# Encoder layer with a routed mixture of experts: combine weights applied per slot, residual built by accumulating DMAs, two experts combined by one-hot matmuls

## The chip, the cores and the metric

The kernel runs on one core of a Trainium2 chip. The metric is the device time of one execution in microseconds (us), the median of several runs; lower is better.

## The reference, cut to what matters

512 tokens of width 1024 pass through a gated attention and gating stage, a cross-attention over 256 memory rows, a mixture of 16 experts and a last normalization. The change touches the mixture and what follows it. Each token picks one group of four experts and two experts in it; an expert is a SwiGLU block of inner width 512, and its output is scaled by a combine weight of the token:

```python
ew = jax.nn.softmax(evals, axis=-1) * gval
expert_id = gidx * EXPERTS_PER_GROUP + eidx
combine = jnp.sum(jax.nn.one_hot(expert_id, N_EXPERTS) * ew[..., None], axis=1)
for e in range(N_EXPERTS):
    he = jax.nn.silu(t @ w_gate[e]) * (t @ w_up[e])
    y = y + combine[:, e:e + 1] * (he @ w_down[e])
...
return rms_norm(x, g_final)
```

## The kernel before, in words

All engines follow an order written out by hand (a manual schedule): each engine runs its instructions in the order in which the program records them, and a wait holds back all that stands behind it on that engine.

**One expert.** Up to 128 rows of an expert's tokens are gathered from `h3d` in HBM. Precision comes from splitting each fp32 operand into a high part (`h`, made by ScalarE, L128) and a low part (`l`, the difference, made by VectorE or, for one of twelve pieces of an expert, by GpSimd, L129) and running three matmuls (L237 to L239). An expert has six weight chunks of 1 MB (gate 0 and 1, up 2 and 3, down 4 and 5), each in two halves; each half feeds six matmuls of 128x512. `W.pump` converts the next half whenever a half has been used, six slots ahead; `W.issue` loads chunks into raw slots as these come free.

**A period.** `expert_period(e)` records the gate and up matmuls of expert e (`gate_up`, eight halves; hooks (j, i) run small work after chunk j, half i), then the transposes of the next expert's rows (`xtr`: eight transposes `pt_xt` in two banks, copied to `xh` and `xl`), then the down matmuls of expert e-1 (`down_scatter`: four halves into `y`, which is scattered to `ybuf` in HBM by an indirect DMA of GpSimd, L1205). Hook (0, 1) transposes the SwiGLU result of expert e-1 (`h_e`: `pt_h`, `hh`, `hl`). For the row numbers of an expert, VectorE builds a one-hot matrix (`oh_e`, L1171), four small matmuls contract it with `vals` (`ids_e`, L1178), and VectorE writes `ixall` (L1179), whose columns are the row in `h3d` and the row in `ybuf`. Row numbers are made four experts ahead and gathers three ahead. All transposes and the `ids` results use the two PSUM banks of tag T in turn: a new one waits until the one two before it has been read.

**The end.** A token's two outputs lie in a low and a high row of `ybuf`, unscaled. After the scatter of expert 14, four loads of 1 MB bring `ybuf` back (`yt`, L1385); ScalarE, GpSimd and VectorE scale and add the low half into the residual `xr`; for the high half eight groups of matmuls add `yt` (through an fp32 identity, L1435) and expert 15's output (through its transposed one-hot `ohT`, L1439, L1440), and VectorE scales by `whi` and adds (L1444). Sums of squares, a reciprocal root by small VectorE steps (L253 to L282, in two chains), products by GpSimd (L1453) and the stores follow. `combine_weights` (14 small VectorE operations) stands in expert 5's period.

Of the kernel before, what the change touches and what calls it, by code (L numbers as in the profile page):

```python
# [12 lines left out]
I32 = mybir.dt.int32  # L13
# [20 lines left out]
AHEAD = 4  # L34
# [8 lines left out]
def encoder(ctx, tc, x, mem, wf, we, wr, br, gv, gcol, gqk, rope, lngb, wsT, bs, out):  # L43
# [1172 lines left out]
    def ids_e(e):  # L1216
        ixs[e] = ids(f"e{e}", ohs[e], lambda t: vals[:, t, e, :], ixall[:, e])
# [3 lines left out]
    W.limit = len(W.order) - 1  # L1221
# [5 lines left out]
    ids_e(1)  # L1227
# [7 lines left out]
    wlo = rt_([P, NT], "wlo")  # L1235
    whi = rt_([P, NT], "whi")
# [7 lines left out]
    def combine_weights():  # L1244
# [43 lines left out]
    def down(e, evac, pumps=(1, 1, 1, 1)):  # L1288
        for n in range(2):
            c = cid[e, 4 + n]  # L1290
            ps = bank("F", f"y{n}_e{e}")
# [9 lines left out]
    def down_scatter(e, pumps=(1, 1, 1, 1)):  # L1301
        if e == 4:
            yt = W.take("y12", [P, 2, D])
            ys.extend(yt[:, i] for i in range(2))
        y = ys[e % len(ys)]
        down(e, lambda n, ps: A.activation(y[:, n * 512:(n + 1) * 512], ps, AF.Copy), pumps)  # L1306
        s_ = scatter(f"e{e}", y, ixs[e])
# [9 lines left out]
    def expert_period(e):  # L1317
        gu_banks(e)
        if e == 5:
# [5 lines left out]
        def oh_ids(n, a, b):  # L1325
            hooks[a].append(lambda: oh_e(n))
            hooks[b].append(lambda: ids_e(n))

        if e == 0:
            def second():  # L1330
                ids_e(2)
                gather(ixs[2], xes[0])

            hooks[0, 0] = [lambda: oh_e(2)]
            hooks[2, 0] += [counts]
            hooks[2, 1] = [second, lambda: oh_e(3)]
# [16 lines left out]
        if e + 3 < NE:  # L1353
# [329 lines left out]
```

## Time and profile before

| what | value |
|---|---|
| median of 3 runs | 792.25 us (792.01 to 792.33) |
| profiled execution, its own time | 791.65 us |
| span of its trace | 789.9 us |
| PE (TensorE matmul) busy | 738.5 us, 93% |
| PEld (weight load) busy | 615.0 us, 78% |
| DVE (VectorE) busy | 610.6 us, 77% |
| ACT (ScalarE) busy | 462.9 us, 59% |
| POOL (GpSimd) busy | 183.7 us, 23% |
| moved by DMA | 163.72 MB, 207 GB/s |

The span is divided into what happens up to 457 us (all before the experts), the expert periods from 457 to 752.8 us, and the end from there to 789.9 us. The share of busy time is a mean over all of it; what an edit is worth has to be read from the stage in which it stands. An engine's idle time is named with the event that ended it.

### The profile page before, as it was taken

Reading aid. Unit: us, or ns where it says so; the run is one execution under the profiler, and the core shown is the slowest. Engines: PE = TensorE matmul, PEld = TensorE weight load, DVE = VectorE, ACT = ScalarE, POOL = GpSimd, SP = SyncE. Lnnn points to the kernel's source line nnn. Section 1 sums busy time; section 2 is a strip of 40 time slices with the busy share of each in tenths; the row PEclk is TensorE's granted clock in tenths of the full one; section 3 lists DMA queues with packets and bytes.
Section 4 is the critical chain, followed back from the end, with each engine's and each line's share of the span. In section 5 each row is a group of like instructions: output and inputs, shape, how many; then the busy total and the mean of one; then the engine's idle time right before and its main releaser. Section 6 shows DMA issues by size and latency. Waiting matters only on the chain.

```text
span 789.9 us, 10636 instructions
## 1 busy us (share of the span) xinstructions
PE 738.5 (93%) x3895; PEld 615.0 (78%) x3896; DVE 610.6 (77%) x1030; ACT 462.9 (59%) x703; POOL 183.7 (23%) x133
## 2 busy tenths in 40 slices
PE   4987999999999999999999989999999999999990
PEld 3775899778888888889988867888788878888760
DVE  5869899989563424658776878899999999999765
ACT  4544767665422323235555446888788888888732
POOL 4425322222000010102222120333333333322131
PEclk9989999999999999999999999999999999999996
DMA  7303221111133326436634369999899999993352
GB/s 285 134 1 126 88 107 54 55 54 54 54 106 107 107 102 244 138 115 254 245 107 187 134 246 420 420 419 396 326 398 370 372 365 373 380 379 133 108 216 110
DMA packets 28813, 163.72 MB, mean 207 GB/s; under 512 B 5077, under 2 KB 5109, under 8 KB 12496
## 3 DMA queue, kind: packets, MB, share of 16 engines
q1 hardware_dynamic: 20384, 140.52, 46.3%
q0 software_dynamic: 7360, 19.29, 6.7%
q10 hardware_dynamic: 1008, 3.15, 1.0%
q8 instruction: 33, 0.54, 0.3%
q14 instruction: 28, 0.23, 0.1%
HBM read 154.63 MB, written 16.25 MB: 216 GB/s over the span
## 4 chain that ended last, share of the span: by engine, by line
PE 71%; DVE 17%; ACT 6%; issue 3%; DMA 2%; SPq 0%; DVEq 0%; ACTq 0%
PE u_e L237 4%; PE y_e L237 3%; PE y_e L239 3%; PE y_e L238 3%; PE u_e L238 3%; PE u_e L239 3%; PE g_e L238 3%; PE g_e L237 3%; PE g_e L239 3%; PE g L238 3%; PE g L239 3%; PE g L237 3%; DVE l_e L129 2%; PE y L238 2%; PE y L239 2%
## 5 line engine op out<-in xcount | busy, mean ns | idle before, releaser
L129 DVE TENSOR_TENSOR l_e<-r_e,h_e 128x1024 fp32r<-128x1024 f32 x174 | 222.0, 1320 | 26.4 <-ACT h_e L128 26.3
L128 ACT ACTIVATE h_e<-r_e 128x1024 fp32r<-128x1024 f32 x188 | 191.9, 1055 | 24.5 <-PE u_e L239 12.5
L1183 POOL DMA_INDIRECT xe<-h3d,ixall x15 | 23.0, 1535 | 139.7 <-PE pt_xt_e L296 90.6
L237 PE MATMUL g_e<-h_e,xh_e 128*128 128x512 f32 x124 | 50.9, 411 | 0.0
L237 PE MATMUL u_e<-h_e,xh_e 128*128 128x512 f32 x124 | 50.7, 409 | 0.0
L238 PE MATMUL g_e<-l_e,xh_e 128*128 128x512 f32 x124 | 49.5, 400 | 0.8 <-DVE l_e L129 0.8
L238 PE MATMUL u_e<-l_e,xh_e 128*128 128x512 f32 x124 | 49.5, 399 | 0.0
L239 PE MATMUL u_e<-h_e,xl_e 128*128 128x512 f32 x124 | 49.5, 399 | 0.0
L239 PE MATMUL g_e<-h_e,xl_e 128*128 128x512 f32 x124 | 49.4, 399 | 0.0
L237 PE MATMUL y_e<-h_e,hh_e 128*128 128x512 f32 x120 | 48.7, 406 | 0.7 <-ACT hh_e L231 0.7
L239 PE MATMUL y_e<-h_e,hl_e 128*128 128x512 f32 x120 | 47.5, 396 | 0.0
L238 PE MATMUL y_e<-l_e,hh_e 128*128 128x512 f32 x120 | 47.4, 395 | 0.0
L580 ACT ACTIVATE p<-s,nm,qsc 128x512 f32<-128x512 f32 x32 | 25.1, 784 | 35.5 <-DVE nm L577 20.4
L129 POOL TENSOR_TENSOR l_e<-r_e,h_e 128x1024 fp32r<-128x1024 f32 x14 | 33.5, 2396 | 51.2 <-ACT h_e L128 51.2
L1306 ACT ACTIVATE y<-y_e 128x512 f32<-128x512 f32 x30 | 18.0, 600 | 22.6 <-PE y_e L239 22.6
L1205 POOL DMA_INDIRECT ybuf<-y,ixall x15 | 25.5, 1697 | 24.2 <-ACT y L1306 22.1
L238 PEld LDWEIGHTS g_e<-l_e,xh_e 128*128 128x128 f32 x124 | 23.6, 191 | 6.1 <-DVE l_e L129 1.2
L239 PEld LDWEIGHTS g_e<-h_e,xl_e 128*128 128x128 f32 x124 | 23.6, 190 | 6.1 <-DVE xl_e L232 0.4
L239 PEld LDWEIGHTS u_e<-h_e,xl_e 128*128 128x128 f32 x124 | 23.6, 190 | 5.7
L238 PEld LDWEIGHTS u_e<-l_e,xh_e 128*128 128x128 f32 x124 | 23.6, 190 | 5.0
L237 PEld LDWEIGHTS g_e<-h_e,xh_e 128*128 128x128 f32 x124 | 23.7, 191 | 5.0
L237 PEld LDWEIGHTS u_e<-h_e,xh_e 128*128 128x128 f32 x124 | 23.6, 190 | 5.0
(451 smaller groups left out, 2159.9 us busy)
## 6 DMA issues: line engine op xcount, KB each, us to landing
r_e<-in_we_dram SPq DMA_DIRECT2D x95, 1024.0 KB, 9.1
r_a<-in_wf_dram SPq DMA_DIRECT2D x4, 1024.0 KB, 5.0
r_b<-in_wf_dram SPq DMA_DIRECT2D x4, 1024.0 KB, 4.7
r_y<-in_wf_dram SPq DMA_DIRECT2D x4, 1024.0 KB, 4.8
r_wo<-in_wf_dram SPq DMA_DIRECT2D x4, 1024.0 KB, 4.8
ybuf<-zt POOLq DMA_DIRECT2D x2, 2048.0 KB, 12.8
yt<-ybuf SPq DMA_DIRECT2D x4, 1024.0 KB, 10.9
xt<-in_x_dram SPq DMA_DIRECT2D x4, 512.0 KB, 7.5
```

Source lines behind the costliest of these rows:

```text
L128: A.activation(h, rr, AF.Copy)
L129: lo = lambda X=G if onpool >> i & 1 else V, l=l, rr=rr, h=h: X.tensor_tensor(l, rr, h, op=ALU.subtract)
L237: T.matmul(ps, ah, bh, start=first and i == 0, stop=False)
L238: T.matmul(ps, ah, bl, start=False, stop=False)
L239: T.matmul(ps, al, bh, start=False, stop=last and i == n - 1)
L580: A.activation(pr, ps, AF.Exp, bias=nm, scale=qsc[t][:, h:h + 1], accum_out=sx)
L1183: G.indirect_dma_start(out=xe, out_offset=None, in_=h3d, in_offset=bass.IndirectOffsetOnAxis(ap=ix[:, 0:1], axis=0), bounds_check=S - 1, o ...
L1205: return G.indirect_dma_start(out=ybuf, out_offset=bass.IndirectOffsetOnAxis(ap=ix[:, 1:2], axis=0), in_=y, in_offset=None, bounds_check=2 ...
L1306: down(e, lambda n, ps: A.activation(y[:, n * 512:(n + 1) * 512], ps, AF.Copy), pumps)
```

## The change

- The combine weight is applied per slot of an expert (`wsl`, one column per expert) when `y` leaves PSUM, by the scale operand of that copy. The weights travel through the `ids` matmuls: `vals` gets three more fp16 columns (a weight in three pieces), and `slot_weights` adds the pieces by four small VectorE operations.
- `combine_weights` (now 6 operations) and `weight_tables` (17 small GpSimd operations) stand in expert 1's period. Experts 0 to 3 (`NLATE`) have had their row numbers before that: their `y` stays in one of three buffers, and two periods later `late` builds the one-hot again, contracts it (`weight_of`), scales `y` on ScalarE and scatters it.
- Row numbers are made and rows gathered two experts ahead, both at hook (2, 1) of a period.
- After expert 13's scatter eight DMAs of 512 KB on GpSimd's queue add `ybuf` into `xr` (`accum_op`), first the low rows and then the high ones. The loads `yt`, the scatter of expert 14, the identity matmuls and the scaled adds are gone.
- Experts 14 and 15 are both combined by one-hot matmuls. Expert 14's part for the columns 0 to 511 is put ahead of and between the transposes of expert 15's SwiGLU result. One chain of reciprocal-root steps serves all four row tiles; the products that GpSimd made are made by VectorE.

```diff
-    def ids(name, oh, val_t, ix):
+    def slot_weights(name, pi, e):
+        sw = sm.tile([P, 3], F32, tag="sw", bufs=2, name=f"sw_{name}")
+        V.tensor_copy(sw, pi[:, 2:5])
+        for i in (1, 0):
+            V.scalar_tensor_tensor(sw[:, i:i + 1], sw[:, i + 1:i + 2], 1.0 / WK, sw[:, i:i + 1], op0=ALU.mult, op1=ALU.add)
+        V.tensor_scalar(wsl[:, e:e + 1], sw[:, 0:1], 1.0 / WS, None, op0=ALU.mult)
+
+    def ids(name, oh, e, ix, n=2):
         pi = bank("T", f"ids_{name}")
         for t in range(NT):
-            T.matmul(pi[:, :2], oh[:, t], val_t(t), start=t == 0, stop=t == NT - 1)
+            T.matmul(pi[:, :n], oh[:, t], vals[:, t, e, 0:n], start=t == 0, stop=t == NT - 1)
         V.tensor_scalar(ix, pi[:, 0:2], BIGI, None, op0=ALU.add)
+        if n > 2:
+            slot_weights(name, pi, e)
...
+    def weight_of(e):
+        pi = bank("T", f"wt_e{e}")
+        for t in range(NT):
+            T.matmul(pi[:, 2:5], ohs[e][:, t], vals[:, t, e, 2:5], start=t == 0, stop=t == NT - 1)
+        slot_weights(f"e{e}", pi, e)
...
+    def late(e):
+        weight_of(e)
+        A.activation(ye[e], ye[e], AF.Copy, scale=wsl[:, e:e + 1])
+        y_scatter(e)
...
+        def ids_g(n, k=5):
+            ids_e(n, k)
+            gather(ixs[n], xes[n % 2])
         if e == 0:
...
-            hooks[2, 1] = [second, lambda: oh_e(3)]
-            hooks[3, 0] = [lambda: ids_e(3), lambda: xT.update({1: xtr("e1", xes[1], xslot)}), lambda: oh_e(0)]
-        elif e + AHEAD < NE:
...
-        if e == 5:
-            hooks[3, 1] = [combine_weights]
+            hooks[2, 1] = [lambda: ids_g(2, 2), lambda: oh_e(3)]
+            hooks[3, 0] = [lambda: xT.update({1: xtr("e1", xes[1], xslot)})]
+            hooks[3, 1] = [lambda: oh_e(0)]
+        elif e == 1:
+            hooks[0, 0] += [lambda: ids_g(3, 2)]
+            hooks[1, 0] += [lambda: ids_e(0, 2)]
+            hooks[1, 1] += [combine_weights, weight_tables]
+        elif e + 2 < NE:
+            hooks[0, 1].append(lambda: oh_e(e + 2))
+            hooks[2, 1].append(lambda: ids_g(e + 2))
+        if 2 <= e < 2 + NLATE:
+            hooks[1, 0].append(lambda: oh_e(e - 2))
+            hooks[3, 0].append(lambda: late(e - 2))
         if e == NE - 2:
             W.climit = 2 * cid[e, 4] + 3
+            hooks[1, 1].append(lambda: oh_tr(0))
...
+    for i in range(2):
         for t in range(NT):
+            G.dma_start(xr[:, t, :], ybv[t][:, i], accum_op=ALU.add)
     h_e(E - 1)
...
-    down_scatter(E - 1, (1, 1, 0, 0))
+    down(E - 1, evac(0), (1, 1, 0, 0))
...
-        nc.sync.dma_start(yt, ybv[t])
...
+    def comb(t, n, i):
+        cs = slice(n * 512, (n + 1) * 512)
+        for j in range(2):
+            T.matmul(yc[t, n], ohT["t"][:, i, t], yhl[i][:, j, cs], start=i == 0 and j == 0, stop=i == 1 and j == 1)
...
     for i in range(2):
+        comb(2 * i, 0, 0)
+        comb(2 * i + 1, 0, 0)
...
-        V.scalar_tensor_tensor(xr[:, t, cs], yc[n, t], whi[:, t:t + 1], xr[:, t, cs], op0=ALU.mult, op1=ALU.add)
+        V.tensor_tensor(xr[:, t, cs], yc[t, n], xr[:, t, cs], op=ALU.add)
+        A.activation(sqj[:, cs], xr[:, t, cs], AF.Square, accum_out=ssf[:, n, t:t + 1])
...
+    V.tensor_tensor(yos[3], xr[:, 3, :], gfin, op=ALU.mult)
+    V.tensor_tensor(ssf[:, 0], ssf[:, 0], ssf[:, 1], op=ALU.add)
+    rs = rsqrt(ssf[:, 0], 1.0 / D, EPS, NT, "fin")
+    store(3, rs[:, 3:4], True, q=A)
+    store(0, rs[:, 0:1])
+    store(1, rs[:, 1:2])
+    store(2, rs[:, 2:3], n=2)
```

What this moves stands below at three places. First VectorE at the end of expert 0's period, where expert 1's rows are transposed (`ixall` is the reading of a row-number bank, `xl` that of a transpose bank). Before:

```order
L1179 TENSOR_SCALAR ixall<-ids_e_4718 128x2
L1171 TENSOR_TENSOR oh_e_4727<-io_3529,posm 128x512
L129 TENSOR_TENSOR l_e_1_4736<-r_e_1_4221,h_e_1_4735 128x1024
L1179 TENSOR_SCALAR ixall<-ids_e_4741 128x2
L232 TENSOR_TENSOR xl_e_4748<-pt_xt_e_4749,xh_e_4747 128x512
```

Now:

```order
L1190 TENSOR_SCALAR ixall<-ids_e_4717 128x2
L1171 TENSOR_TENSOR oh_e_4726<-io_3529,posm 128x512
L129 TENSOR_TENSOR l_e_1_4735<-r_e_1_4221,h_e_1_4734 128x1024
L232 TENSOR_TENSOR xl_e_4741<-pt_xt_e_4742,xh_e_4740 128x512
L232 TENSOR_TENSOR xl_e_4741<-pt_xt_e_4749,xh_e_4740 128x512
```

The second `ixall` (expert 3's row numbers) has moved from behind the low-part operation into expert 1's period, and with it the bank that the second four transposes had to wait for.

Second, VectorE at the end of the period of expert 2, the first with a late expert (`sw` and `wsl` are `slot_weights`, `wt_e` is the bank of `weight_of`; `l_e_5` is a half of chunk 5, `l_e_0` the first half of the next expert). Before:

```order
L129 TENSOR_TENSOR l_e_5_5051<-r_e_5_4683,h_e_5_5050 128x1024
L1179 TENSOR_SCALAR ixall<-ids_e_5054 128x2
L129 TENSOR_TENSOR l_e_5_5067<-r_e_5_4683,h_e_5_5066 128x1024
L129 TENSOR_TENSOR l_e_0_5079<-r_e_0_4695,h_e_0_5078 128x1024
L1283 TENSOR_TENSOR g_5042<-g_5042,u_e_4974 128x512
```

Now:

```order
L129 TENSOR_TENSOR l_e_5_5053<-r_e_5_4682,h_e_5_5052 128x1024
L1190 TENSOR_SCALAR ixall<-ids_e_5056 128x2
L1181 COPY sw_e_5062<-ids_e_5056 128x3
L1183 SCALAR_TENSOR_TENSOR sw_e_5062<-sw_e_5062 128x1 x2
L1184 TENSOR_SCALAR wsl<-sw_e_5062 128x1
L129 TENSOR_TENSOR l_e_5_5077<-r_e_5_4682,h_e_5_5076 128x1024
L1181 COPY sw_e_5087<-wt_e_5082 128x3
L1183 SCALAR_TENSOR_TENSOR sw_e_5087<-sw_e_5087 128x1 x2
L1184 TENSOR_SCALAR wsl<-sw_e_5087 128x1
L129 TENSOR_TENSOR l_e_0_5103<-r_e_0_4694,h_e_0_5102 128x1024
```

Eight small operations have come between low parts, the last four behind the low part of the half `l_e_5_5077`.

Third, ScalarE at the same place, now:

```order
L128 ACTIVATE h_e_5_5052<-r_e_5_4682 128x1024
L128 ACTIVATE h_e_5_5076<-r_e_5_4682 128x1024
L1339 ACTIVATE y_4645<-y_4645,wsl 128x1024
L128 ACTIVATE h_e_0_5102<-r_e_0_4694 128x1024
L231 ACTIVATE xh_e_5107<-pt_xt_e_5109 128x512
```

The scaling of the late `y` (L1339) reads `wsl` and stands ahead of the high part `h_e_0_5102`, which the low part `l_e_0_5103` of the fence before reads; before, the high parts followed one another there.

## Rows read from the trace of the kernel before

**Rows 1.** Windows: length, busy of PE PEld DVE ACT POOL; clock, DMA share, GB/s

```profile
544.90:563.30 18.40, 18.40 (x90) 14.78 (x89) 17.08 (x18) 15.03 (x19) 5.96 (x4) 1.00 1.01 384
563.30:582.60 19.30, 18.52 (x89) 14.65 (x88) 19.06 (x32) 15.03 (x19) 5.91 (x3) 1.00 0.84 329
...
674.30:692.40 18.10, 18.10 (x85) 14.75 (x84) 16.76 (x16) 14.95 (x19) 5.93 (x3) 1.00 1.01 381
...
752.80:789.90 37.10, 17.01 (x60) 10.84 (x60) 23.34 (x42) 12.91 (x20) 10.48 (x4) 0.79 0.38 149
```

**Rows 2.** Timeline of one steady period: start, length, operation, idle before it and releaser

```profile
599.67 1.04 PE L296 MATMUL pt_xt_e<-identf,xe 128*128 128x128 f32 x8
...
615.00 0.25 PE L1178 MATMUL ids_e<-vals,oh_e 128*128 128x2 f16 x4
618.00 1.04 PE L296 MATMUL pt_xt_e<-identf,xe 128*128 128x128 f32 x8
...
606.07 4.85 DVE L129 TENSOR_TENSOR l_e<-r_e,h_e 128x1024 fp32r<-128x1024 f32 x3 [1.31 <-ACT h_e L128]
610.85 0.68 DVE L1171 TENSOR_TENSOR oh_e<-io,posm 128x512 f16<-128x512 bf16 x1
...
613.18 4.62 DVE L129 TENSOR_TENSOR l_e<-r_e,h_e 128x1024 fp32r<-128x1024 f32 x4
617.72 0.15 DVE L1179 TENSOR_SCALAR ixall<-ids_e 128x2 int32<-128x2 f32 x1
...
606.84 2.94 ACT L128 ACTIVATE h_e<-r_e 128x1024 fp32r<-128x1024 f32 x3
```

**Rows 3.** Timeline around the transposes of expert 1's rows, DVE, ACT, PE

```profile
471.40 0.15 DVE L1179 TENSOR_SCALAR ixall<-ids_e 128x2 int32<-128x2 f32 x1
...
467.39 1.28 ACT L1279 ACT_TABLE_LOAD   x1
...
471.61 1.11 PE L296 MATMUL pt_xt_e<-identf,xe 128*128 128x128 f32 x4 [3.44 <-DVE ixall L1179]
...
475.08 0.63 PE L237 MATMUL g_e<-h_e,xh_e 128*128 128x512 f32 x1
...
488.67 1.03 PE L296 MATMUL pt_xt_e<-identf,xe 128*128 128x128 f32 x8
```

**Rows 4.** Window there, PE alone: length, PE busy, granted clock, DMA share, GB/s

```profile
473.00:475.00 2.00, 2.00 (x6) 0.50 0.98 410
```

**Rows 5.** Timeline of the end, by PE, DVE and ACT

```profile
760.60 1.02 PE L1435 MATMUL yc<-yt,identf 128*128 128x512 f32 x2
...
770.92 0.40 PE L1440 MATMUL yc<-yhl,ohT 128*128 128x512 f32 x1
...
768.17 2.36 DVE L282 TENSOR_SCALAR v_fin<-ssf 128x2 f32<-128x2 f32 x1
...
772.28 2.37 DVE L264 SCALAR_TENSOR_TENSOR p_fin<-t_fin 128x2 f32<-128x2 f32 x1
...
778.97 0.16 DVE L1509 TENSOR_TENSOR ssf<-ssf 128x1 f32<-128x1 f32 x1 [0.82 <-ACT yt L1448]
...
780.94 1.42 DVE L1462 SCALAR_TENSOR_TENSOR yt<-xr,y_fin,xe 128x512 f32<-128x512 f32 x2
...
758.50 1.15 ACT L1395 ACTIVATE yt<-yt,wlo 128x1024 f32<-128x1024 f32 x1
```

**Rows 6.** DMA issues, two stretches: kind, count, KB each, median us to landing

```profile
yt<-ybuf SPq DMA_DIRECT2D x4, 1024.0 KB, 10.9
...
ybuf<-y,ixall POOLq DMA_INDIRECT x4, 3.9
...
xr<-in_x_dram POOLq DMA_DIRECT2D x4, 512.0 KB, 6.4
```

**Rows 7.** GpSimd's indirect DMAs to ybuf: the last but one; all, min/median/max

```profile
734.89 0.98 POOL L1205 DMA_INDIRECT ybuf<-y,ixall  x1 [15.78 <-ACT y L1306]
...
L1205 POOL DMA_INDIRECT ybuf<-y,ixall x15: 974/1806/1821, 496.8 to 742.2; - x15
```

More of the change, by code (lines that the diff above doesn't have):

```diff
@@ L1286, in h_e, with down @@
         hT[e] = htr(f"e{e}", gs[e])
-    def down(e, evac, pumps=(1, 1, 1, 1)):
+    def down(e, evac, pumps=(1, 1, 1, 1), banks=None):
         for n in range(2):
             c = cid[e, 4 + n]
-            ps = bank("F", f"y{n}_e{e}")
+            ps = banks[n] if banks else bank("F", f"y{n}_e{e}")
             for i in range(2):
@@ L1299, in encoder, with y_scatter @@
     ys = [mo.tile([P, D], F32, tag="y", bufs=1, name="y0")]
[L1301 to L1307, printed above, removed]
+    ye = {}
+    def y_scatter(e):
+        s_ = scatter(f"e{e}", ye[e], ixs[e])
         for o in scat:
@@ L1310, in down_scatter @@
         scat.append(s_)
+    def down_scatter(e, pumps=(1, 1, 1, 1)):
+        if e == 0:
+            yt = W.take("y12", [P, 2, D])
+            ys.extend(yt[:, i] for i in range(2))
+        y = ye[e] = ys[e % len(ys)]
+        sc = {} if e < NLATE else {"scale": wsl[:, e:e + 1]}
+        down(e, lambda n, ps: A.activation(y[:, n * 512:(n + 1) * 512], ps, AF.Copy, **sc), pumps)
+        if e >= NLATE:
+            y_scatter(e)
+    def late(e):
+        weight_of(e)
+        A.activation(ye[e], ye[e], AF.Copy, scale=wsl[:, e:e + 1])
+        y_scatter(e)
     gps = {}
@@ L1352, in expert_period, with oh_tr @@
             xT[e + 1] = xtr(f"e{e + 1}", xes[(e + 1) % 2])
-        if e + 3 < NE:
-            gather(ixs[e + 3], xes[(e + 1) % 2])
         if e:
             down_scatter(e - 1, (1,) * 4 if e < NE - 2 else (1, 1, 0, 0))
+    ohT = {}
+    def oh_tr(i):
+        pt = bank("T", f"ohT{i}", (P, NT, P))
+        for t in range(NT):
+            T.matmul(pt[:, t, :], ohs[NE - 2 + i][:, t], identb, start=True, stop=True)
+        if i == 0:
+            ohT["t"] = W.spare("ohT", [P, 2, NT, P], F32R)
+        A.activation(ohT["t"][:, i], pt, AF.Copy)
     for e in range(NE - 1):
@@ L1362, in encoder, with evac, fn @@
     gu_banks(E)
-    ohT = {}
-    def oh_tr():
-        pt = bank("T", "ohT", (P, NT, P))
+    yhl = [None, None]
+    def evac(i):
+        w = wsl[:, NE - 2 + i:NE - 1 + i]
+        yhl[i] = W.spare(f"yhl{i}", [P, 2, D], F32R)
+        def fn(n, ps):
+            cs = slice(n * 512, (n + 1) * 512)
+            if i and n:
+                comb(0, 0, 1)
+            A.activation(yhl[i][:, 0, cs], ps, AF.Copy, scale=w)
+            if i and n:
+                addc(0, 0)
+            V.scalar_tensor_tensor(yhl[i][:, 1, cs], ps, w, yhl[i][:, 0, cs], op0=ALU.mult, op1=ALU.subtract)
+        return fn
+    ybv = ybuf.rearrange("(s t p) d -> t p s d", s=2, p=P)
+    for i in range(2):
         for t in range(NT):
-            T.matmul(pt[:, t, :], ohs[E][:, t], identb, start=True, stop=True)
-        ohT["t"] = W.spare("ohT", [P, NT, P], F32R)
-        A.activation(ohT["t"], pt, AF.Copy)
+            G.dma_start(xr[:, t, :], ybv[t][:, i], accum_op=ALU.add)
     h_e(E - 1)
@@ L1463, in store @@
             q.dma_start(ov[:, t, cs], jk)
[L1465 to L1512 removed]
+    down(E, evac(1), banks=yE)
+    for t in range(1, NT):
+        comb(t, 0, 1)
+        addc(t, 0)
+    yc[0, 1], yc[1, 1], yc[2, 1], yc[3, 1] = (bank("TTSO"[t], f"yc{t}_1") for t in range(NT))
+    for t in range(3):
+        comb(t, 1, 0)
+    for t in range(NT):
+        if t == 3:
+            comb(3, 1, 0)
+        comb(t, 1, 1)
+        addc(t, 1)
+    V.tensor_tensor(yos[3], xr[:, 3, :], gfin, op=ALU.mult)
[5 more added lines that the diff above has]
+    store(2, rs[:, 2:3], n=2)
     manual.close()
@@ L1563, in overflow_block @@
         oh = onehot(f"o{b}", pe)
[L1564 removed]
+        ix = ids(f"o{b}", oh, 0, sm.tile([P, 2], I32, tag="ix", bufs=1, name=f"ix_o{b}"))
         gather(ix, xo)
```

177 lines of the change are left out of this document (42 added, 135 removed).

## The prediction

> **What bounds the kernel now.** I read the table of windows first. In a steady expert period TensorE is busy for all of it: 18.40 of 18.40 us [rows 1]. From one set of row transposes to the next is 618.00 - 599.67 = 18.33 us [rows 2]; the period without row numbers takes 18.10 [rows 1]. The periods are bound by TensorE, but VectorE is close behind: busy 17.08 of 18.40, its spare one gap of 1.31 us in which it waits for a ScalarE high part [rows 1, 2]. How thin that is shows the period with `combine_weights`: VectorE is busy 19.06 instead of 17.08, TensorE idles 0.8, and the period takes 19.30, so 2.0 us more for VectorE cost 0.9 [rows 1].
>
> The timeline shows that VectorE also lags inside a period. The row numbers' matmuls end about 615.2, and VectorE reads them at 617.72, only 0.28 ahead of the transposes that need the bank [rows 2]. At expert 1 this lag already bites: the second four transposes wait 3.44 us for `ixall` at 471.40, because that reading stands behind a low part whose high part stands behind a ScalarE table load of 1.28 us [rows 3]. After it the granted clock is 0.50, the 1.2 GHz level [rows 4].
>
> The end takes 789.9 - 752.8 = 37.1 us and is bound by TensorE and then VectorE [rows 1, 5].
>
> **The change, part by part.**
>
> *Start of the experts: -4.4.* Expert 3's row numbers leave the place between expert 1's transposes, so all eight run in one go from about 467.5, and six up matmuls follow to about 469.8. Then a smaller wait takes over: ScalarE's order is unchanged, so VectorE's `xl` still starts after the low part that ended about 471.4 (`ixall` stood right behind it [rows 3]), and is there at 472.1. The third matmul of expert 1, the first to need `xl`, ran at 475.08 + 2 x 0.43 = 475.9 and now runs at 472.1: 3.8 us. The next three slow matmuls gain 0.2 each. A new wait of some 0.5 (the transposes of expert 0's result, whose product on VectorE is now just in time) stands against one set of row-number matmuls less. I take 4.4. Ends: 1.9, if the shorter idle time brings the half clock too (stall and half clock together cost 3.4 + 11 x 0.2 + 0.3 = 5.9, of which the clock is 2.5), and 5.9, if no wait takes its place.
>
> *Late experts, four periods: +11.7.* A late period adds to VectorE one one-hot matrix (0.68) and two `slot_weights`. Each of those is four operations that depend on one another; the ten dependent ones from 778.97 to 780.94 take 0.20 each [rows 5], so about 0.7 per set. Together 2.0 us, on 17.1: VectorE needs 19.1 of an 18.33 us period. What is worse is the order. ScalarE's scaling of `y` waits for `wsl`, and VectorE's next operation after `wsl` is the low part whose high part stands behind that scaling. Both queues are in order, so VectorE idles for the scaling (1.15, as the same form takes [rows 5]) and one high part (2.94 / 3 = 0.98 [rows 2]), 2.2 us with the two handshakes. The old gap of 1.31 does not add, since VectorE is late by then. A late period is so 19.1 + 2.2 = 21.3, some 21.4 with bubbles, or +3.05.
>
> TensorE feels it where the transposes wait for their banks. With `weight_of` there are two banks to be read ahead of them, and the second is read behind one more low part (4.62 / 4 = 1.15 [rows 2]): in the first late period at about 617.72 + 0.68 + 0.7 + 1.15 + 0.2 = 620.4 on the steady period's clock, against 618.44 + 0.2 (its four extra matmuls) when the second four transposes want it. So +1.8 in the first, 3 x 3.05 in the next, and some 0.7 while the lag is worked off after: 11.7. Ends: 4 x 1.0 = 4, the price of 2.0 us of VectorE time in the `combine_weights` period; and 11.7 + 3 x 2.5 = 19, if TensorE's idle time of about 2.9 per late period brings the half clock each time, at the price of the start.
>
> *Half clock in late periods: +1.* Between 0 and 7.5 (just derived). VectorE sets the pace there, so slower matmuls first eat TensorE's own idle time; I take 1.
>
> *`combine_weights` moved: -1.0.* Its period falls from 19.30 to 18.33. In expert 1's period, which loses a set of row numbers, six operations and 17 small GpSimd ones are covered by VectorE's gap; without that cover they would cost what they cost now, 1.0.
>
> *Other periods: +0.6.* Periods 12 and 13 get row numbers again, 18.30 for 18.10: +0.4. Expert 14's one-hot transposes add four small matmuls, +0.2. One `slot_weights` per period (0.7) fits VectorE's gap of 1.31; if the gap were gone, eight periods would pay 0.7. The gathers have 18 us to land. The raw slot that the `y` buffers take four periods earlier costs nothing while high parts follow one another without a wait for a weight load, as they do [rows 2].
>
> *The end: -7.0.* Now TensorE spends from 760.60 to 770.92 plus its last matmul on eight groups, 1.32 us each [rows 5], VectorE adds, and two of its tiny steps take 2.36 and 2.37 us in place of 0.17 while GpSimd multiplies [rows 5]; it ends at 780.94 + 1.42 = 782.4. After the change, counted from 752.8: eight combining matmuls come ahead of expert 15's down matmuls, mostly where TensorE waited (+0.4), so those end at 761.2. Then two combining matmuls 0.5, one add 0.7 and one low part 0.7 to 763.1; seven adds of 0.65 to 767.6 (the 22 other matmuls at 0.233 are done by 767); one product 1.15; the root chain 2.0 to 770.8; stores of 1.3, 1.3, 0.65 and 0.75 to 774.7. That is 7.7 less. Against it, all 2 MB of output now leave after 772, half of which was gone before: 0.7. Ends: 4 if the outputs queue, 8.5 if not.
>
> *Accumulating DMAs: 0.* Expert 13's scatter is issued at 734.89 and lands some 3.9 later [rows 6, 7], at 738.8. The sum is needed for the first tile at 761.9 and for the last at 764.4. No row has an accumulating DMA. Plain loads on the same queue bring 4 x 512 KB in 6.4 [rows 6], two dependent rounds 12.8; the 4 MB of `yt` came in 10.9 [rows 6]. If the reading of the destination doubles it, 25.6, done at 764.4: just in time. That is the middle I take. Ends: 10.9, and 8 x 6.4 = 51 if each waits for the one before.
>
> An indirect DMA of GpSimd took 0.98 at 734.89 and 1.81 in the median of all [rows 7]; the new ones are issued just after the short one, so I add nothing. The Trainium skill's "SBUF — State Buffer" (Who interferes with whom) reads a GpSimd-issued DMA that seems stalled by VectorE as one whose descriptor generation was starved of port time. By that rule VectorE's work there would stretch eight issues by up to 0.8 each, and the sums could come some 6 us late; that belongs to rival 2.
>
> **Sum.** -4.4 + 11.7 + 1.0 - 1.0 + 0.6 - 7.0 + 0 = +0.9. The profiled execution took 791.65 (span 789.9), 0.6 under the median of 792.25; the sum gives 792.6 there and 793.2 for the median. A measurement of this kernel can tell about 0.2%, 1.6 us, from no change, so the forecast is **no change that can be told**: two gains at the ends, eaten by the late experts in the middle.
>
> **Rivals.**
> 1. *The late weights hide in the six-slot lead* (faster). For it: the one period with 2.0 us more for VectorE lost only 0.9. Against: that period had no ScalarE operation between VectorE and VectorE, and no second bank to be read. Four periods at 1.0 give 4 in place of 11.7 + 1: 793.2 - 8.7 = 784.5.
> 2. *The accumulating DMAs land late* (slower). VectorE's first add waits for them, and all of the end behind it. It decides from 25 us on for the eight. At thrice the plain rate, 3 x 12.8 = 38, the last tile is there at 777 and not 764.4: +13, 806. For it: two rounds, both streams through one queue, stretched issues. Against: DMA is otherwise idle there.
> 3. *TensorE falls to the lower clock more often* (slower): at the start (+2.5) and in two late periods more (+2.5): 798. For it: idle 3.44 was followed by 0.50 [rows 3, 4].
>
> **How the numbers follow.** The forecast's case 0.5, rival 1 0.22, rival 2 0.18, rival 3 0.10. The forecast's own range is the ends of its surest terms, some 788 to 798: within it 0.13 faster by over 0.2%, 0.22 within, 0.15 slower. Rival 1 is all faster, rival 2 all slower, rival 3 0.07 slower and 0.03 within. Sum: faster 0.35, same 0.25, slower 0.40. Both signs hold most of it, hence the range 785 to 801; under it lies a part of rival 1, above it most of rival 2, together less than 0.2.
>
> **What would show it.** In the new profile: the second four transposes of expert 1 without their 3.44 wait, and the next set near 484; four periods of about 20.2, 21.4, 21.4 and 21.4 with TensorE waiting for the reading of `wt_e` and VectorE for ScalarE; 18.3 in the others; an end of about 30 instead of 37 us; the first add right after its matmuls. Wrong would be: late periods under 19.5, or an add into `xr` that waits for a DMA.

## The result, and the profile after

The changed kernel takes **801.4 us** (median of 4 runs, 801.04 to 801.76) against 792.13 for the kernel before on the same chip: ratio 1.0121, 95% interval 1.0103 to 1.0138. It is slower by 1.2%. The forecast was 793.2, no change that can be told; the time lies just above the range of 785 to 801. The profiled execution took 801.04, its span 799.2.

The windows of the profile after, stretch by stretch (length, busy of PE, PEld, DVE, ACT, POOL; granted clock, DMA share, GB/s). They answer to [rows 1]:

```profile
468.80:485.40 16.60, 14.86 (x77) 11.20 (x76) 13.44 (x22) 12.87 (x16) 7.30 (x4) 1.00 1.01 421
485.40:513.10 27.70, 20.59 (x94) 16.20 (x93) 18.99 (x27) 14.75 (x18) 17.05 (x19) 0.88 1.01 417
534.60:556.50 21.90, 18.94 (x93) 14.66 (x93) 19.37 (x27) 15.56 (x19) 5.00 (x3) 1.00 0.84 308
578.40:598.00 19.60, 18.48 (x88) 14.77 (x88) 17.10 (x21) 17.31 (x21) 5.66 (x3) 1.00 0.85 290
634.90:653.30 18.40, 18.40 (x89) 14.73 (x89) 17.85 (x22) 15.30 (x18) 5.48 (x3) 1.00 0.99 373
...
770.40:799.20 28.80, 13.31 (x60) 10.50 (x59) 16.98 (x32) 10.88 (x23) 0.14 (x1) 0.77 0.50 136
```

Read the first column first. The second row is the surprise: one period of 27.7 us, 7.1 of it with TensorE idle, while GpSimd, busy for 5 to 7 us in the other periods, is busy for 17.05. The late period in the third row is 21.9 long, where 21.4 was forecast; the plain one is 18.4; the end is 28.8 instead of 37.1.

Periods are measured here from the start of the second four row transposes of one expert to that of the next. Those of expert 2 start at 485.39 now and started at 489.11 before, the last up matmul ends at 770.39 and ended at 752.77. So the whole difference of the two spans, 9.3 us, comes apart like this:

| term, as the prediction put it | forecast | measured |
|---|---|---|
| everything ahead of the experts (nearly the same code; over the traces of e1 to e7 it varies by 0.9) | 0 | +0.9 |
| start of the experts | -4.4 | -4.6 |
| expert 2's period, the first late one | +1.8 | **+9.4** |
| the three late periods after it, with the half clock | +9.15 + 1.0 | +10.3 |
| expert 6's period: lag worked off, `combine_weights` gone | +0.7 - 1.0 | +0.3 |
| other periods | +0.6 | +1.3 |
| the end | -7.0 | -8.3 |
| sum | +0.9 | +9.3 |

One row is wrong by 7.6 us; the others are off by 0.2 to 1.3, in both directions. The timeline around the wrong one, the profile after, PE, POOL and DVE (start, length, operation, idle time before it and what ended it):

```profile
494.54 0.48 PE L237 MATMUL g_e<-h_e,xh_e 128*128 128x512 f32 x1
502.13 0.79 PE L238 MATMUL g_e<-l_e,xh_e 128*128 128x512 f32 x1 [7.11 <-POOL l_e L129]
502.72 0.63 PE L239 MATMUL g_e<-h_e,xl_e 128*128 128x512 f32 x1
...
482.91 3.64 POOL L1274 TENSOR_SCALAR lgt<-io,i,gval 128x16 f32<-128x16 f32 x1 [3.70 <-DVE gval L1269]
486.55 1.28 POOL L1275 TENSOR_SCALAR hi<-io,i,d 128x16 f32<-128x16 f32 x1
487.82 0.41 POOL L1274 TENSOR_SCALAR lgt<-io,i,gval 128x16 f32<-128x16 f32 x1
...
498.36 1.10 POOL L1279 CAST vals<-hi 128x64 f16<-128x64 f32 x1
499.30 2.77 POOL L129 TENSOR_TENSOR l_e<-r_e,h_e 128x1024 fp32r<-128x1024 f32 x1
...
482.91 4.62 DVE L129 TENSOR_TENSOR l_e<-r_e,h_e 128x1024 fp32r<-128x1024 f32 x4
```

TensorE waits 7.11 us for a low part that GpSimd makes. GpSimd starts it at 499.30, the moment the last of the 17 operations of `weight_tables` ends; the first began at 482.91. Nothing else stands between. The next matmuls take 0.63 instead of 0.39: the granted clock is 0.50, the 1.2 GHz level, from 499.5 to 506.3. The window there, PE alone (length, PE busy; granted clock, DMA share, GB/s):

```profile
499.50:506.30 6.80, 4.17 (x10) 0.50 1.01 412
```

The late periods went as the prediction described them, 0.1 to 0.6 us longer than it had them. The second of the three, profile after, PE, DVE, ACT:

```profile
554.75 0.63 PE L296 MATMUL pt_xt_e<-identf,xe 128*128 128x128 f32 x4 [1.85 <-issue]
556.49 0.66 PE L296 MATMUL pt_xt_e<-identf,xe 128*128 128x128 f32 x4 [1.11 <-DVE sw_e L1181]
...
556.86 0.15 DVE L1184 TENSOR_SCALAR wsl<-sw_e 128x1 f32<-128x1 f32 x1
559.17 1.23 DVE L129 TENSOR_TENSOR l_e<-r_e,h_e 128x1024 fp32r<-128x1024 f32 x1 [2.17 <-ACT h_e L128]
...
557.04 1.15 ACT L1339 ACTIVATE y<-y,wsl 128x1024 f32<-128x1024 f32 x1 [6.28 <-DVE wsl L1184]
558.10 1.04 ACT L128 ACTIVATE h_e<-r_e 128x1024 fp32r<-128x1024 f32 x1
```

`wsl` is ready at 557.0, ScalarE scales `y` (1.15), then makes the high part (1.04), and VectorE stands idle for 2.17 us: the 2.2 of the prediction. TensorE waits for both banks, 1.85 and 1.11. (The profile names no releaser for the first wait; VectorE's copy out of the row-number bank ran from 554.50 to 554.65, just ahead of it.)

The end and the accumulating DMAs, profile after, timeline by DVE and POOL:

```profile
778.75 0.69 DVE L1465 TENSOR_TENSOR xr<-yc,xr 128x512 f32<-128x512 f32 x1 [1.64 <-PE yc L1443]
780.02 4.42 DVE L1465 TENSOR_TENSOR xr<-yc,xr 128x512 f32<-128x512 f32 x7
784.47 1.22 DVE L1492 TENSOR_TENSOR yo<-xr,xe 128x1024 f32<-128x1024 f32 x1
787.91 3.81 DVE L1477 SCALAR_TENSOR_TENSOR yo<-xr,y_fin,xe 128x1024 f32<-128x1024 f32 x4
...
756.34 3.64 POOL L1422 DMA_DIRECT2D xr<-ybuf  x4 [2.81 <-DMA ybuf<-y,ixall]
762.00 0.84 POOL L1422 DMA_DIRECT2D xr<-ybuf  x1 [2.02 <-DMA xr<-ybuf]
```

The first add follows its matmul, not a DMA. The second round of sums is issued transfer by transfer as the first lands; the last of the eight lands at 779.36, 23.0 us after the first was issued at 756.34.

### The profile page after: what moved, and what is told of

Same layout as the page of the kernel before. It is cut to its first block, busy times and chain, and to the rows that moved or that the text cites. A ratio compares the mean times of both kernels' runs of the same rounds, so it can differ in the third digit from the quotient of the medians.

```text
span 799.2 us, 10761 instructions
## 1 busy us (share of the span) xinstructions
PE 740.8 (93%) x3915; PEld 616.7 (77%) x3916; DVE 619.4 (78%) x1082; ACT 467.0 (58%) x711; POOL 188.6 (24%) x152
## 4 chain that ended last, share of the span: by engine, by line
PE 61%; DVE 22%; ACT 8%; issue 5%; DMA 3%; SPq 0%; DVEq 0%; ACTq 0%
DVE l_e L129 5%; PE g L237 3%; PE g L238 3%; PE g L239 3%; PE y_e L237 3%; PE y_e L239 3%; PE y_e L238 2%; PE g_e L239 2%; PE g_e L237 2%; PE u_e L237 2%; PE g_e L238 2%; PE u_e L239 2%; PE u_e L238 2%; DMA r_e<-in_we_dram 2%; ACT h_e L128 2%
## 5 line engine op out<-in xcount | busy, mean ns | idle before, releaser
L129 DVE TENSOR_TENSOR l_e<-r_e,h_e 128x1024 fp32r<-128x1024 f32 x174 | 225.2, 1337 | 28.2 <-ACT h_e L128 27.9
L129 POOL TENSOR_TENSOR l_e<-r_e,h_e 128x1024 fp32r<-128x1024 f32 x14 | 37.7, 2693 | 53.3 <-ACT h_e L128 46.9
L1196 POOL DMA_INDIRECT xe<-h3d,ixall x15 | 16.4, 1096 | 130.4 <-DVE sw_e L1183 111.4
L1218 POOL DMA_INDIRECT ybuf<-y,ixall x14 | 21.1, 1509 | 27.5 <-ACT y L1333 15.7
L237 PEld LDWEIGHTS y_e<-h_e,hh_e 128*128 128x128 f32 x120 | 23.0, 192 | 5.7 <-ACT hh_e L231 1.1
L239 PEld LDWEIGHTS y_e<-h_e,hl_e 128*128 128x128 f32 x120 | 22.9, 191 | 5.8 <-DVE hl_e L232 0.4
L129 DVE TENSOR_TENSOR l_wo<-r_wo,h_wo 128x1024 fp32r<-128x1024 f32 x8 | 9.8, 1226 | 22.6 <-ACT h_wo L128 22.6
```

Source lines behind the costliest of these rows:

```text
L129: lo = lambda X=G if onpool >> i & 1 else V, l=l, rr=rr, h=h: X.tensor_tensor(l, rr, h, op=ALU.subtract)
L237: T.matmul(ps, ah, bh, start=first and i == 0, stop=False)
L239: T.matmul(ps, al, bh, start=False, stop=last and i == n - 1)
L1196: G.indirect_dma_start(out=xe, out_offset=None, in_=h3d, in_offset=bass.IndirectOffsetOnAxis(ap=ix[:, 0:1], axis=0), bounds_check=S - 1, o ...
L1218: return G.indirect_dma_start(out=ybuf, out_offset=bass.IndirectOffsetOnAxis(ap=ix[:, 1:2], axis=0), in_=y, in_offset=None, bounds_check=2 ...
```

## The experiments

After the result there were two theories. **A**: GpSimd's queue is the loss; the tables hold up a low part that TensorE needs, and everything else went as forecast. **B**: the late work fills those periods anyway, and the low part was only the last of several things to be late. The runs e1 and e5 part these two. The other runs have an A and a B of their own, which their expectations name: e2 and e6 take the late period apart, e3 and e7 test two terms that were forecast, and e4, e8, e9 and e10 look for the place where the weights are cheap. All times are medians with the ratio to the kernel before on the same chip; e1 to e4, e5 to e8, and e9 and e10 ran on three different chips, so that across these groups the ratios are what compares.

**e1: the low part off GpSimd.**

```diff
-            W.order.append((we[e, j], f"e{e}_{j}", 4, int(j == POOLJ and 0 < e < NE - 1)))
+            W.order.append((we[e, j], f"e{e}_{j}", 4, int(j == POOLJ and 0 < e < NE - 1 and e != 2)))
```

> The changed kernel with one edit: expert 2's low part of the third gate half goes to VectorE instead of GpSimd, so that nothing TensorE needs stands behind the 17 weight-table operations on GpSimd (482.9 to 499.5 us in the changed kernel). Theory A (GpSimd's queue): the 7.11 us wait of TensorE at expert 2's third gate half goes, and the half clock that follows it; from one second set of row transposes to the next expert 2's period falls from 27.7 to some 20 us, as the prediction had it; time 801.4 - 7.5 = about 794. Rival B (the late work on VectorE and ScalarE fills that period anyway, the low part was only the last of several things to be late): the wait moves to another operation and the time stays above 799.

Measured: 794.33 us, ratio 1.0037 (1.0025 to 1.0050). Windows of e1, and the two waits of TensorE that are left in expert 2's period:

```profile
485.60:505.70 20.10, 18.79 (x94) 14.82 (x92) 19.59 (x25) 14.67 (x18) 16.44 (x18) 1.00 1.01 420
505.70:527.60 21.90, 18.99 (x92) 14.71 (x92) 19.38 (x26) 15.57 (x19) 5.06 (x3) 1.00 1.00 411
```

```profile
501.72 0.24 PE L1189 MATMUL ids_e<-vals,oh_e 128*128 128x5 f16 x4 [1.11 <-POOL vals L1279]
...
505.75 0.66 PE L296 MATMUL pt_xt_e<-identf,xe 128*128 128x128 f32 x4 [0.25 <-DVE sw_e L1181]
```

Expert 2's period is 20.1 instead of 27.7, at full clock, though GpSimd still spends 16.44 us on its work there. That is A: with nothing urgent queued behind them the tables cost little. They are not free: the row numbers' matmuls are the next in line to want them, and wait 1.11 us. So it is in part a coincidence that the period comes out at the forecast's +1.8: the forecast had TensorE wait for the second bank, and here that wait is only 0.25. VectorE copies that bank out at 505.54, so without the first wait the second would presumably be longer by as much; no run separates the two. The late periods are unchanged.

**e2: the scaling behind the next high part** (on top of e1; `late` without `weight_of`).

```diff
-            hooks[3, 0].append(lambda: late(e - 2))
+            hooks[3, 0].append(lambda: weight_of(e - 2))
+            hooks[3, 1].append(lambda: late(e - 2))
```

> e1 with one more edit: in the four late periods the weights are still computed after the first half of the fourth weight chunk, but ScalarE's scaling of y and its scatter are put after the second half, behind the next high part. Theory A (the chain VectorE weights -> ScalarE scaling -> high part -> VectorE low part costs 2.2 us per late period): the late periods fall from 21.9 to 20.2 us, 4 x 1.2 to 1.7 = 5 to 7 us less than e1, about 788. Rival B (the second bank to be read and VectorE's 2.0 us more work set the late period by themselves): the late periods stay within 0.5 us of e1's, time within 2 us of e1.

Measured: 789.25 us, ratio 0.9980 (0.9965 to 0.9995); 5.1 under e1. The same place in e2's timeline, DVE, ACT, PE:

```profile
546.52 0.15 DVE L1184 TENSOR_SCALAR wsl<-sw_e 128x1 f32<-128x1 f32 x1
546.60 1.23 DVE L129 TENSOR_TENSOR l_e<-r_e,h_e 128x1024 fp32r<-128x1024 f32 x1
...
546.71 1.16 ACT L1338 ACTIVATE y<-y,wsl 128x1024 f32<-128x1024 f32 x1 [3.20 <-DVE wsl L1184]
...
546.15 0.65 PE L296 MATMUL pt_xt_e<-identf,xe 128*128 128x128 f32 x4 [1.11 <-DVE sw_e L1181]
```

The low part now follows `wsl` at once and the scaling runs beside it. The late periods fall from 21.92, 21.97 and 21.93 to 20.27, 20.42 and 20.42, and the one after them from 19.87 to 18.34. So A: 1.5 to 1.65 us of each late period was the place of the scaling in ScalarE's queue (the scatter behind it moves too). Two stretches of half clock went as well: e1 had the granted clock at 0.50 at 527.8 to 531.3 and 572.2 to 575.6, where TensorE had idled 1.8 and 1.1 us a short time apart; e2, with 0.4 and 1.1, has no such stretch among its late periods. The first of them cost little: e1's late period that holds it took 21.97 us, the two without 21.92 and 21.93. Expert 2's period grew from 20.13 to 20.83, as its row numbers now wait 2.21 us for the tables.

**e6: one-hot matrices kept** (on top of e2: the second `oh_e` of experts 0 to 3 is dropped, the first has a buffer of its own, two `y` buffers instead of three).

> e2 with one more edit: the one-hot matrices of experts 0 to 3 are kept and not made again, which takes 0.68 us of VectorE out of each late period and leaves everything else. Theory A (with the scaling out of the way a late period is as long as VectorE's work in it): 20.4 - 0.7 = 19.7 us per late period, e2's time less 4 x 0.7 = 2.8, about 786.5. Rival B (the order decides: the second bank is read behind one more low part, whatever VectorE does before): late periods stay at 20.3 to 20.5, time within 1 us of e2.

Measured: 789.37 us, ratio 0.9972 (0.9959 to 0.9986). By these times e6 and e2 can't be told apart; single runs spread from 786.4 to 790.4 and from 787.3 to 792.8. The traces tell more. The windows of the second late period of e2 and of e6, in this order:

```profile
525.70:546.10 20.40, 18.90 (x92) 14.71 (x92) 18.91 (x26) 15.93 (x19) 4.44 (x3) 1.00 0.98 379
```

```profile
525.40:545.20 19.80, 18.69 (x92) 14.69 (x92) 18.28 (x26) 15.92 (x19) 4.44 (x3) 1.00 0.98 382
```

0.63 us less of VectorE made the period 0.6 shorter, three times over, as A had it. Expert 2's period took 0.5 of that back: it came to the row numbers earlier and waited 2.73 us for the tables instead of 2.21.

**e5: the tables on VectorE** (the 17 `G.` calls of `weight_tables` become `V.`).

> The changed kernel with one edit: the 17 weight-table operations run on VectorE instead of GpSimd; expert 2's low part stays on GpSimd. Theory A (what stood ahead of the low part in GpSimd's queue was the whole loss): the 7.11 us wait goes as it did in e1, expert 2's period 20 to 21 us; VectorE takes 17 x 0.16 to 0.23 = about 3 us more in expert 1's period, where it had gaps; time 794 to 797. Rival B (a small operation is as dear on VectorE, and TensorE then waits for VectorE's low parts): expert 2's period stays above 23 us and the time above 798.

Measured: 795.79 us, ratio 1.0062 (1.0045 to 1.0078). The 7.11 us wait is gone here too, with the low part still on GpSimd; GpSimd now stands idle until that part's high part is there. Expert 2's period is 22.25, longer than expected. Window of that period and GpSimd's timeline in e5:

```profile
485.00:507.30 22.30, 19.59 (x95) 14.46 (x93) 21.95 (x34) 14.83 (x18) 3.53 (x2) 1.00 1.02 421
```

```profile
490.82 2.53 POOL L129 TENSOR_TENSOR l_e<-r_e,h_e 128x1024 fp32r<-128x1024 f32 x1 [11.96 <-ACT h_e L128]
```

The same 17 operations run on VectorE from 482.57 to 486.60, 4.0 us, where GpSimd took 16.5; VectorE is busy for nearly all of the period that follows, 21.95 of 22.30.

**e3: only the start** (in the kernel before).

```diff
-            hooks[3, 0] = [lambda: ids_e(3), lambda: xT.update({1: xtr("e1", xes[1], xslot)}), lambda: oh_e(0)]
+            hooks[3, 0] = [lambda: xT.update({1: xtr("e1", xes[1], xslot)})]
+            hooks[3, 1] = [lambda: oh_e(0)]
...
             if e == 1:
+                hooks[0, 0] += [lambda: ids_e(3), lambda: gather(ixs[3], xes[1])]
...
-        if e + 3 < NE:
+        if e and e + 3 < NE:
```

> The kernel before with one part of the change: expert 3's row numbers and their gather leave the place between expert 1's transposes and go behind the first half of expert 1's own gate, and expert 0's one-hot matrix goes half a chunk later. Everything else, the end too, is the kernel before. Theory A (the start is worth 4.4 us by itself): the 3.44 us wait goes, about 787.7. Rival B (the time saved is lost again in expert 1's period, where TensorE meets weights or VectorE that are no earlier than before): within 1.5 us of the kernel before, 791 to 793.

Measured: 788.32 us, ratio 0.9963 (0.9949 to 0.9977): 2.9 under the kernel before by the medians, 3.9 by the two traces at expert 2's row transposes (485.26 against 489.11). A, if a little short of 4.4: this part of the change is a gain by itself, and the wait for the high and low halves of the rows (0.92 and 0.64 us) takes the place of the 3.44, as forecast.

**e4: four weights at once.** On top of e1, the core of the edit:

```diff
-NLATE = 4
+NLATE = 1
...
+    def weights_of():
+        pi = bank("T", "wt", (P, 4, 4))
+        for e in range(4):
+            for t in range(NT):
+                T.matmul(pi[:, e, 0:3], ohs[e][:, t], vals[:, t, e, 2:5], start=t == 0, stop=t == NT - 1)
...
-            hooks[1, 1] += [combine_weights, weight_tables]
...
-        if 2 <= e < 2 + NLATE:
-            hooks[1, 0].append(lambda: oh_e(e - 2))
-            hooks[3, 0].append(lambda: late(e - 2))
+        if e == 2:
+            hooks[3, 0].append(weights_of)
+            hooks[3, 1].append(lambda: late(0))
```

`combine_weights` goes to expert 0's period, `weight_tables` to the start of expert 1's, behind the gather for expert 3.

> The changed kernel with three edits: expert 2's low part on VectorE as in e1; the combine weights and GpSimd's tables made some 8 us earlier; and the weights of experts 0 to 3 made together in expert 2's period from kept one-hot matrices (16 small matmuls into one bank, four VectorE operations), so that experts 1 to 3 are weighted as they leave PSUM and only expert 0's result is scaled late. Theory A (the late periods cost what their order on VectorE and ScalarE costs): no period of 21.9 us is left, all after expert 2's are 18.4, expert 2's at most 20; 801.4 - 7.5 - 11 = about 783. Rival B (the weights of one expert more per period, which stay, and the accumulating DMAs take the gain: the sums land at 779.4 in the changed kernel, 0.6 us after the first add, and a kernel that gets there 18 us earlier is bound by them): about 788 or more, with the first add waiting on a DMA.

Measured: **781.88 us**, ratio 0.9882 (0.9865 to 0.9898): faster than both kernels. Windows of e4: expert 2's period, a plain one, the end:

```profile
484.20:503.40 19.20, 18.92 (x107) 15.02 (x105) 18.65 (x25) 15.65 (x19) 12.47 (x14) 1.00 1.01 420
...
613.70:632.10 18.40, 18.40 (x89) 14.75 (x89) 17.86 (x22) 15.26 (x18) 5.53 (x3) 1.00 0.97 364
...
749.20:778.30 29.10, 13.35 (x60) 10.51 (x59) 16.97 (x32) 10.87 (x23) 0.18 (x1) 0.80 0.51 136
```

No late period is left, expert 2's is 19.2, all others 18.4 or less, and the end keeps its 29. The first add again waits for its matmul, not for a DMA.

**e7: plain loads** (e4 without `accum_op`; the sums are left out).

> e4 with plain loads in place of the eight accumulating ones: the sum with the residual and with the other half is left out. Theory A (the accumulating transfers are hidden and cost the time nothing): the landings come closer together than the 2.5 us of e4, some 1.6 us apart as 2 MB in 6.4 us would have it, and the time stays within 1.5 us of e4's 781.9. Rival B (they land last: in e4 the last sum is there 1.7 us after the first add began): the adds start earlier and the time falls by more than 1.5 us.

Measured: 780.95 us, ratio 0.9871 (0.9854 to 0.9887), which can't be told from e4. The issues of e7, then of e4 (count, KB each, median us from issue to landing):

```profile
xr<-ybuf POOLq DMA_DIRECT2D x8, 512.0 KB, 6.5
```

```profile
xr<-ybuf POOLq DMA_DIRECT2D x8, 512.0 KB, 9.7
```

The second round of loads lands 1.3 us apart, still closer than the 1.6 expected; the accumulating ones landed 2.2 to 2.8 us apart in the changed kernel, 2.5 in the mean, and 2.5 to 3.4 in e4. The accumulation is dearer, and hidden: A.

**e8: no late weight at all**: weights and tables on VectorE in expert 0's period, every expert's weights with its row numbers.

> The changed kernel with the combine weights and the tables made on VectorE in expert 0's period, so that every expert's weights come with its row numbers and nothing is scaled late (expert 1's one-hot matrix is kept, and its weights are made in its own period). Theory A (VectorE has room in expert 0's period: 16.9 us busy of 21.6 in e4): no period of 19.2 or longer, all of 18.4, time 0.8 under e4, about 781. Rival B (VectorE runs without a gap from 458 to 468 there, so 3 us more of it come out at expert 1's row transposes and the first up matmuls): TensorE waits some 2 to 3 us more at 470, time 783 to 785.

Measured: 788.44 us, ratio 0.9957 (0.9941 to 0.9974): 6.6 over e4 by the medians, some 6 by the ratios. B, and worse than B had it. Timeline of e8, PE and DVE:

```profile
474.72 0.25 PE L1189 MATMUL ids_e<-vals,oh_e 128*128 128x5 f16 x4 [7.50 <-DVE cmax L1161]
...
468.82 2.32 DVE L1275 TENSOR_SCALAR hi<-io,i,d 128x16 f32<-128x16 f32 x1
471.05 0.28 DVE L1274 TENSOR_SCALAR lgt<-io,i,gval 128x16 f32<-128x16 f32 x1
```

VectorE reaches the weights only at 467.2, behind its low parts, and ends the tables at 474.7; TensorE reaches the row numbers that read them at 467.2 and waits for all of it (the profile names `cmax`, a small step right behind the tables that ends within 0.02 us of them). From expert 2's period on all are 18.25 to 18.46 long: without late work nothing is lost there, but this place costs more than that saves.

**e9: expert 1's low part on VectorE too** (on top of e4, `2 < e` in the condition of e1).

> e4 with one edit: expert 1's low part too goes from GpSimd to VectorE. In e4 a one-hot matrix on VectorE (two inputs in SBUF) takes 2.65 us instead of 0.68 while GpSimd's low part runs beside it (467.2 to 469.6), right ahead of the low halves of expert 1's rows, for which TensorE waits 0.69 us. Theory A (the two engines keep each other out while both read from SBUF): the one-hot matrix takes 0.7, VectorE is 2.0 - 1.2 = 0.8 us ahead, TensorE's second wait shrinks from 0.69 to 0.3 or less, time 0.3 to 0.7 under e4's 781.9. Rival B (the one-hot matrix is long for another reason, such as its place or its data): it stays at 2.65, VectorE is 1.2 later, time 1 us over e4.

Measured: 782.94 us, ratio 0.9898 (0.9883 to 0.9912): no gain, 1.1 over e4 by the medians, with intervals that overlap. Timeline of e4, the one-hot matrix and GpSimd's low part, and of e9:

```profile
467.47 2.65 DVE L1171 TENSOR_TENSOR oh_e<-io,posm 128x512 f16<-128x512 bf16 x1
...
467.18 2.39 POOL L129 TENSOR_TENSOR l_e<-r_e,h_e 128x1024 fp32r<-128x1024 f32 x1 [6.73 <-ACT h_e L128]
```

```profile
467.23 1.23 DVE L129 TENSOR_TENSOR l_e<-r_e,h_e 128x1024 fp32r<-128x1024 f32 x1 [1.25 <-ACT h_e L128]
...
469.74 0.68 DVE L1171 TENSOR_TENSOR oh_e<-io,posm 128x512 f16<-128x512 bf16 x1
...
469.88 0.66 PE L296 MATMUL pt_xt_e<-identf,xe 128*128 128x128 f32 x4 [2.11 <-DVE ixall L1190]
```

The mechanism of A is there: without GpSimd beside it the one-hot matrix takes 0.68. The time is not: the low part that was moved stands in VectorE's queue ahead of the weights and the row numbers, waits 1.25 us for its high part, and TensorE waits 2.11 for what stands behind. Once more a queue, this time one I had put there.

**e10: the weights earlier still**: exponentials and weights ahead of expert 0's row splits, the tables on GpSimd right after the gather for expert 1, all four weights in expert 1's period.

> e4 with the weights earlier: the exponentials and combine weights ahead of expert 0's row splits (VectorE waits there 0.9 us for ScalarE), GpSimd's tables right after expert 1's gather, the weights of experts 0 to 3 together in expert 1's period, so that nothing is scaled late; expert 1's low part on VectorE, expert 2's on GpSimd again. Theory A (GpSimd has 17 us for the tables from 460 on, when nothing that TensorE needs stands behind them but the gather for expert 2, wanted at 483): expert 2's period 18.3 instead of 19.2, time 0.9 to 1.5 under e4, about 780.5. Rival B (beside VectorE's low parts the tables take over 20 us; the gather for expert 2 or the weights' matmuls come late): TensorE waits at the weights' matmuls or at expert 2's row transposes, time 782 or more.

Measured: 787.85 us, ratio 0.9961 (0.9948 to 0.9973): 6 over e4, B. Timeline of e10, PE and POOL:

```profile
488.90 1.94 PE L296 MATMUL pt_xt_e<-identf,xe 128*128 128x128 f32 x8 [6.08 <-DMA xe<-h3d,ixall]
...
478.05 1.38 POOL L1274 CAST vals<-hi 128x64 f16<-128x64 f32 x1
479.46 2.08 POOL L1196 DMA_INDIRECT xe<-h3d,ixall  x1
```

The tables take 460.3 to 479.4, 19 us, and the gather for expert 2, whose row numbers were there by 467, goes out behind them. The loss of the change has come back with another instruction in the low part's place.

## Why the prediction was wrong, and where it was right

**The step that failed** is one sentence of the part on `combine_weights`: that in expert 1's period "six operations and 17 small GpSimd ones are covered by VectorE's gap". The cover that it names is one for the six alone. The 17 run on another engine, whose queue I did not follow: I gave them no duration, and did not ask what stood behind them there. They took 16.5 us, and behind them stood a low part that TensorE wanted at 495.0 and that, with its own 2.77, came at 502.1. e1 takes that low part out of the queue and the period falls to 20.1; e5 takes the tables out, and the wait goes too; e10 puts another instruction behind them, and TensorE waits 6.08 for that one. This is shown three times over, and it accounts for 7.6 of the 8.4 us between the sum and the trace.

The duration could have been estimated. In the profile before, two of VectorE's small operations took 2.36 and 2.37 us in place of 0.17 while GpSimd multiplied [rows 5]: I used that to price the end, and did not turn it round. GpSimd's multiplications there, profile before:

```profile
764.76 5.74 POOL L1453 TENSOR_TENSOR yt<-xr,xe 128x1024 f32<-128x1024 f32 x2 [2.66 <-DVE xr L1444]
772.26 2.37 POOL L1453 TENSOR_TENSOR yt<-xr,xe 128x1024 f32<-128x1024 f32 x1 [1.76 <-DVE t_fin L257]
```

VectorE's 2.36 at 768.17 and 2.37 at 772.28 [rows 5] end with them, within 0.03 us. With VectorE busy for nearly all of a period, seventeen small operations of GpSimd that each let one low part of 1.2 us pass give an estimate of some 20 us for the tables.

**Start of the experts**, -4.4: measured -4.6 in the change, -3.9 in the trace of e3, where it stands alone. Right, with its new waits (0.94 for the high and 0.64 for the low halves).

**Late experts**, +11.7 and +1 for the clock: right in mechanism and nearly in size. In e1, free of most of the other loss, the five periods from expert 2's on stand 1.8, 3.6, 3.6, 3.6 and 1.5 us over 18.33, in all 14.2. The mis-sized parts are the lag worked off after (1.5 for 0.7) and each late period (3.6 for 3.05; VectorE was busy for 19.37 us of it, where the working had 19.1). The +1 for the clock did not show: in the change the late period from 556.49 on holds the stretch of half clock and took 21.94 us, the one before it holds none and took 21.92. The chain through ScalarE is shown by e2 (1.5 us a period) and VectorE's own work by e6 (0.6 us for 0.63). Rival 1, that the late weights hide, is out.

**`combine_weights` moved**, -1.0: right. In e2, where hardly a lag is left, its old period takes 18.34 instead of 19.38. In the change the lag of the late periods falls into the same place, so that the two together show +0.3.

**Other periods**, +0.6: +1.3. Periods 12 to 14 cost 0.3 each, where 0.2 each was forecast; a plain period with its `slot_weights` takes 18.42 instead of 18.33, five times. TensorE is busy for all of it in both, so the 0.09 is TensorE's; I did not take it further apart.

**The end**, -7.0: -8.3. The adds were done 14.05 us after the last up matmul where the working had 14.8, and the 0.7 for outputs that queue was not paid: from the last product to the end of the span it is 7.5 us in both kernels. The two operations of 2.36 are 0.17 now.

**Accumulating DMAs**, 0: right. That reading the destination doubles the time of plain loads was an assumption of mine, with no row behind it, and it happened to hold: I took 25.6 us, they took 23.0. e7 shows that plain loads would buy nothing that can be told. The stretched issues that belonged to rival 2 did not come: an accumulating DMA was issued in 0.85 us beside VectorE's low parts (767.52) and in 0.84 with VectorE idle (769.70). Rival 2 is out in this kernel, but with little room: the last sum landed 0.6 us after the first add began, and 1.9 us ahead of the fourth, which by the order of the tiles is the first to need it (780.02 + 2 x 0.63 = 781.28). In e4 that margin is 0.9 us.

**Rival 3**, the lower clock: a stretch of 0.50 did follow the long wait, and one more came in a late period of the change (557.5 to 560.9). The first, ten matmuls at 0.43 instead of 0.23 us from one to the next, added some 2 us to expert 2's period; the second cost nothing that shows. Neither is the cause. At the start the rival did come in one trace: e1 has the granted clock at 0.50 from 473.2 to 476.6, and its start is worth 3.4 us, against 4.6 in the change and in e2, with the same code and the same two waits there.

**What is left of the sum.** The other terms come out near the forecast partly by luck, since their errors cancel. Against the trace before, e1's start is 1.0 us short of the forecast, its five periods with late work and lag cost 1.4 more, the other periods 0.6 more, and the end 1.0 less: 2.9 in all where the sum had 0.9.

## What to carry to other kernels

Work that is free on an idle engine is free only up to the next instruction in that engine's queue: before calling it covered, give it a duration and look up what stands behind it and when that is wanted. Where a late result is scaled by another engine, put the scaling behind whatever feeds the bottleneck, and where several late results need the same small steps, take the steps once for all of them (e4: four in place of sixteen) rather than once per period. e4 made other edits too, so that the worth of this step alone is not shown. An early place is no better than a late one if something urgent is already queued there (e8, e9, e10).

## What the runs showed of the hardware

In the changed kernel a GpSimd operation on 128x16 numbers took 0.41 or 0.42 us while VectorE was idle or ran operations that read one input from PSUM (487.45 to 489.33), and 1.28 to 3.64 us beside VectorE's low parts; the first one took as long as three of them (482.91 to 486.55). It goes the other way too: a one-hot matrix on VectorE took 2.65 instead of 0.68 us beside GpSimd's low part, and was done 0.55 us after that was (e4); e9, without it, shows 0.68. The Trainium skill's "SBUF — State Buffer" (Who interferes with whom) has the rule: a VectorE instruction with two inputs in SBUF contends with a GpSimd instruction that reads SBUF, the lock on the ports that they share is exclusive, and the order of issue decides who blocks. These rows agree with it, in both directions; why the first operation let three low parts pass is not shown. By that rule the tables should be priced by VectorE's instructions beside them and not by their own size, which is what this prediction lacked.

Eight accumulating DMAs of 512 KB landed 2.5 us apart in the mean in the changed kernel, where the second round of plain loads of the same size on the same queue landed 1.3 us apart (e7).
